# The second token block's operand sums in their usual slot, and one more pair of squares on VectorE, in a two-layer encoder kernel

## Chip, core and metric

The kernel runs on one core of one Trainium2 chip. The metric is the device time of one execution in microseconds (us). The time before is the median of three runs, 934.64 us (934.29 to 935.21). Inside a core five engines work side by side, each through its own instructions in the order in which they were written: TensorE (PE in the profile; PEld is its weight load), VectorE (DVE), ScalarE (ACT), GpSimd (POOL) and SyncE (SP, which here only issues transfers). They meet at semaphores alone.

## What is computed

A two-layer encoder trunk on x (512 tokens, 1024 channels), all in fp32, with cross-attention into 256 memory tokens in each layer. The change lies in the start of the first layer, in front of and inside its first product of the normalised x with the input weights. The reference, cut to that:

```python
def rmsnorm(x, g):
    xf = x.astype(jnp.float32)
    y = xf * lax.rsqrt(jnp.mean(xf * xf, axis=-1, keepdims=True) + EPS)
    return (y * g.astype(jnp.float32)).astype(x.dtype)

for i in range(DEPTH):
    h = rmsnorm(x, norm_g[i])
    mem_h = rmsnorm(mem, mem_norm_g[i])
    ...
    proj = jnp.einsum('bsd,de->bse', h, w_in_a[j])     # layer 0
    ...
    o_mem = memory_attention(q_mem, mem_h, w_mem_kv[i], mem_qn_g[i], mem_kn_g[i])
    y = jnp.concatenate([o_mix, o_mem], axis=-1) * jax.nn.silu(gate)
    x = x + jnp.einsum('bse,ed->bsd', y, w_out[i])
```

## The kernel before

**Products.** Every fp32 product is made of three products of rounded operands: each operand is split into a high part (a cast to fp32r) and a low part (the operand minus its high part), and high by high, low by high and high by low are summed in PSUM (`mm_early`, lines 178 and 179, and `mm_late`, line 182). The high part of a weight, `wh`, is a cast on ScalarE (L333; L331 with gains), its low part, `wo`, a subtraction on VectorE (L347; L345 with gains). Both stand in rings of four buffers. Large products are done by Strassen's scheme in Winograd's form: instead of the four quarters of an operand, seven combinations of quarters are multiplied. Those of x are called 12, 11, S1, S2, S4, S3 and 22, in the order of use, and those of the weights 21, 11, T1, T2, 22, T3 and T4. T1 is summed on VectorE (L291), T2 by a transfer that adds T1 into the loaded quarter (L296, issued by POOL).

**x.** The 512 tokens lie in four blocks, `xb[0]` to `xb[3]` (the tiles x_79 to x_82), each with two halves of 512 channels. A block gets its mean square (`norm_1`: two squares with an accumulated sum, L574 on VectorE or L576 on ScalarE, and three small operations on POOL, L578, L535 and L536) and its factor and gain (`norm_2`, L583, VectorE). Blocks 0 and 1 are the upper quarters, 2 and 3 the lower ones. For c = 0 and c = 1, blocks c and 2 + c are transposed on TensorE into the banks of `at` and combined: `first_t` makes 12 and 11 of block c, `diffs_t` makes S1, S3 and keeps 22 of block 2 + c, and `rest_t` makes S2 = S1 - 11 (L675, tile `f11`) and S4 = 12 + S2 (L677, tile `f12`), then writes the two parts of S2, S4, S3 and 22 (`put`: cast L671, subtraction L672). c = 0 and c = 1 are the left and the right 128 columns of one operand tile such as `hS2`.

**Order.** `Driver` is a hand-made schedule. A slot is one group of eight early and four late matmuls. After each slot, tasks whose turn has come run to their next `yield n`, and so put a few instructions on the engines; n is the number of slots to their next turn. What is given to `late` is written at the end of the same slot, what is given to `release` with a delay of one in the next slot, at the point where PSUM banks are handed over (`drv.free()`, behind the group's matmuls and ahead of the weights' work in `W.advance()`). The task `prep` (L1213 on) norms and transposes x; its two tasks `forms(0)` and `forms(1)`, the second one slot behind, run `diffs_t` and `rest_t`.

**Banks.** The product with S2 is added onto the banks that hold the product with 11 (`pj_596` for c = 0, `pj_597` for c = 1). Before that VectorE must have read them into `sn` (L438, the sum for output quarter 11). These two sums are called the banks' sums here.

**Transfers.** SP issues the weights' transfers (L260) in the order of use. Eight semaphores go round, so a transfer is issued only when the one that had its semaphore before has landed.

Of the kernel before, what the change touches and what calls it, by code (L numbers as in the profile page):

```python
# [10 lines left out]
F32 = mybir.dt.float32  # L11
F32R = mybir.dt.float32r
AF = mybir.ActivationFunctionType
ALU = mybir.AluOpType
# [119 lines left out]
def trunk_kernel(ctx: ExitStack, tc: tile.TileContext, x, mem, wall, norm_g, mem_norm_g, gcol,  # L134
                 qn_a, kn_a, qn_b, kn_b, ident_d, mask_d, tab_a, tab_b, out):
    nc = tc.nc
    V, A, G, T = nc.vector, nc.scalar, nc.gpsimd, nc.tensor
# [6 lines left out]
    drv = Driver()  # L144
# [7 lines left out]
    def s2(dt=F32, name="s2"):  # L152
        return pool.tile([128, 512], dt, tag="s2", name=name, bufs=NS2)
# [7 lines left out]
    def sm(n, name):  # L161
        return small.tile([128, n], F32, tag="sm%d" % n, name=name)
# [368 lines left out]
    def rstd_of(ss, n):  # L531

        r = sm(n, "rstd")
        e = sm(n, "mse")
        G.tensor_scalar(e, ss, EPS, None, ALU.add)  # L535
        G.tensor_tensor(r, e, half[:, 0:n], ALU.pow)  # L536
        return r
# [30 lines left out]
    def norm_1(xb, both=False):  # L568

        ss = sm(2, "ss")  # L570
        for j in range(2):
            jk = s2(name="sq")
            if both and j:
                V.tensor_tensor_reduce(jk, xb[j], xb[j], 1.0 / 1024.0, 0.0, ALU.mult, ALU.add, ss[:, j:j + 1])  # L574
            else:
                A.activation(jk, xb[j], AF.Square, scale=1.0 / 32.0, accum_out=ss[:, j:j + 1])  # L576
        r, e = sm(1, "rstd"), sm(1, "mse")
        G.tensor_tensor(e, ss[:, 0:1], ss[:, 1:2], ALU.add)  # L578
        return rstd_of(e, 1)

    def norm_2(xb, r, row, js=(0, 1)):
        for j in js:
            V.scalar_tensor_tensor(xb[j], xb[j], r, row[j], ALU.mult, ALU.mult)  # L583
# [44 lines left out]
    def slot(H, k, c):  # L628
        if c == 0:
            part[k] = big(F32R, "h" + k).rearrange("p (a k t) -> p a k t", a=2, k=4)  # L630
        else:
            H[k] = part[k]
        cs = slice(c * 128, (c + 1) * 128)
        return part[k][:, 0, :, cs], part[k][:, 1, :, cs]
# [9 lines left out]
    def first_t(H, top, c, view=same, turn=same):  # L644

        ps = [(k, turn(turn4(top[j], None, None)), [view(t) for t in slot(H, k, c)]) for k, j in (("12", 1), ("11", 0))]
        for k, p, hl in ps:
            split(*hl, p)
        for k, p, _ in ps:
            A.copy(view(whole(k, c)), p)  # L650

    def diffs_t(H, low, c, view=same, turn=same, late=False):

        f22 = whole("22", c)
        A.copy(view(f22), turn(turn4(low[1], None, None)))
        p = turn(turn4(low[0], None, None))
        yield 1
        s1, s3 = whole("S1", c), whole("S3", c)
        V.tensor_tensor(view(s1), p, view(f22), ALU.subtract)
        V.tensor_tensor(view(s3), view(full["11", c]), p, ALU.subtract)  # L660
        hl = slot(H, "S1", c)
        if late:
            drv.late(lambda: split(*hl, s1))
        else:
            split(*hl, s1)

    def rest_t(H, c, ds, spread=False):

        def put(k, f):
            hi, lo = slot(H, k, c)  # L670
            A.copy(hi, f)  # L671
            (drv.soon if spread and c and k == "S2" else drv.late)(lambda: V.tensor_tensor(lo, f, hi.bitcast(F32), ALU.subtract))  # L672

        s1, s2_, s4, s3, f22 = [full.pop((k, c)) for k in ("S1", "11", "12", "S3", "22")]
        V.tensor_tensor(s2_, s1, s2_, ALU.subtract)  # L675
        if not spread:
            V.tensor_tensor(s4, s4, s2_, ALU.add)  # L677
        put("S2", s2_)
        if spread:
            yield ds[0] - 1  # L680
            V.tensor_tensor(s4, s4, s2_, ALU.add)
            yield 1
        else:
            yield ds[0]
        put("S4", s4)
        yield ds[1]
        put("S3", s3)
        yield ds[2]
        put("22", f22)
        yield 1  # L690
# [24 lines left out]
    def halves(t):  # L715
        return [t[:, 0:512], t[:, 512:1024]]
# [489 lines left out]
    H, H2 = {}, {}  # L1206
# [4 lines left out]
    xb = [halves(t) for t in xt]  # L1211

    n = {}  # L1213

    def prep():

        for c in range(5):
            if c > 2:
                norm_2(xb[c - 1], n[c - 1], rows["x"])
            if 1 < c < 4:  # L1220
                n[c] = norm_1(xb[c], c == 2)
            if 1 < c < 4:
                first_t(H, xb[c - 2], c - 2, by_class, from_rows)
            yield 1

        def forms(c):
            yield from diffs_t(H, xb[2 + c], c, by_class, from_rows, late=True)
            yield 3 + c
            yield from rest_t(H, c, (2 - c, 2, 2))

        drv.spawn(forms(1), 1)
        yield from forms(0)
# [70 lines left out]
    def ahead(u, b):  # L1303

        if (u, b) == (0, 0):
            square(1, 0)
            place_m(1, 0)
            square(0, 1, False)
            W.hi(True)
            W.hi(True)  # L1310
        if (u, b) == (0, 1):
            place_m(0, 1)
            factor(0)
            square(1, 1, False)
            place_m(1, 1)
            n[0] = norm_1(xb[0])
            n[1] = norm_1(xb[1])
            factor(1)
        if (u, b) == (1, 0):
            norm_2(xb[0], n[0], rows["x"])  # L1320
            norm_2(xb[1], n[1], rows["x"])

    drv.spawn(prep(), PD)
    drv.spawn(setup(), SET_AT)
    drv.spawn(masks(), MASK_AT)
# [436 lines left out]
    last_k, both = [], [v[:, :, 256:512] for v in kbT]  # L1762
# [219 lines left out]
```

## Time and profile before

| | |
|---|---|
| median of three runs | 934.64 us |
| the profiled execution's own time | 934.81 us |
| its span in the profile | 933.0 us |
| DVE busy | 800.5 us, 86% of the span |
| ACT busy | 696.6 us, 75% |
| POOL busy | 360.9 us, 39% |
| granted TensorE clock | 1.00 in the whole span |

The 1.8 us between time and span lie ahead of the first and behind the last instruction. A row of the timeline has the start in us, the length in us, engine, line, operation, output <- input, and the count; in brackets it has the idle time just before it and what ended that. The ends of matmuls are modelled and overlap the next start, so what TensorE loses is read from starts.

### The profile page before, as it was taken

The numbers are of one execution on the slowest core, as the hardware profiler recorded it, in microseconds if no ns is written. First come the engines' busy times: TensorE is split into PE (matmuls) and PEld (weight loads), VectorE is DVE, ScalarE is ACT, GpSimd is POOL, SyncE is SP. The second block draws the span as 40 slices with busy tenths as digits, with TensorE's granted clock in tenths as the row PEclk, the third lists the DMA queues.
The fourth block names the chain that finished last, engine by engine and source line by source line (L and its number), as shares of the span: only waits on it lengthen the run. The fifth ranks groups of instructions, "written<-read, shape, count | busy, mean of one in ns | idle before, by whom it ended". The sixth has DMA issues, their size and how long they took to land.

```text
span 933.0 us, 16277 instructions
## 1 busy us (share of the span) xinstructions
PE 925.0 (99%) x5471; PEld 814.4 (87%) x5471; DVE 800.5 (86%) x1453; ACT 696.6 (75%) x1729; POOL 360.9 (39%) x504
## 2 busy tenths in 40 slices
PE   9999999999999999999999999999999999999998
PEld 7879888888888888888889998888988999999886
DVE  6898677878888888979798989999898998789977
ACT  7775789686868686767676767757878887789774
POOL 4411424557564646463746102234252440110122
PEclk9999999999999999999999999999999999999999
DMA  9999947968686868685867899999995677785777
GB/s 349 390 269 331 292 128 191 333 149 243 158 254 158 266 159 272 157 270 115 259 168 213 229 256 274 288 317 330 298 220 114 173 229 187 198 228 116 197 165 181
DMA packets 83179, 212.85 MB, mean 228 GB/s; under 512 B 18960, under 2 KB 25752, under 8 KB 83096
## 3 DMA queue, kind: packets, MB, share of 16 engines
q1 hardware_dynamic: 60744, 141.16, 41.9%
q0 software_dynamic: 20384, 67.12, 39.0%
q10 hardware_dynamic: 1968, 3.54, 1.0%
q8 instruction: 43, 0.70, 0.3%
q14 instruction: 40, 0.33, 0.1%
HBM read 162.96 MB, written 12.65 MB: 188 GB/s over the span
## 4 chain that ended last, share of the span: by engine, by line
PE 88%; DVE 5%; DMA 4%; issue 1%; ACT 1%; POOL 0%; SPq 0%; DVEq 0%; POOLq 0%; ACTq 0%
PE pj L179 23%; PE pj L178 23%; PE pj L182 23%; PE qT L708 2%; DMA wl<-in_wall_dram 2%; PE sa L1468 2%; PE oo L1577 2%; PE ptb L1811 1%; PE sa L1464 1%; DVE wo L347 1%; PE pt L1556 1%; DMA x<-in_x_dram 1%; DMA wl<-wl 1%; PE ob L178 1%; PE ob L182 1%
## 5 line engine op out<-in xcount | busy, mean ns | idle before, releaser
L347 DVE TENSOR_TENSOR wo<-wl,wh 128x1024 fp32r<-128x1024 f32 x253 | 308.5, 1224 | 5.5 <-ACT wh L333 5.5
L333 ACT CAST wh<-wl 128x1024 fp32r<-128x1024 f32 x253 | 267.1, 1061 | 30.5 <-PE pj L179 18.9
L178 PE MATMUL pj<-wh,hS 128*128 128x512 f32 (+1 forms) x416 | 154.6, 380 | 1.1 <-ACT hS L671 1.1
L179 PE MATMUL pj<-wh,hS 128*128 128x512 f32 (+1 forms) x416 | 148.9, 367 | 0.3 <-DVE hS L672 0.3
L178 PE MATMUL pj<-wh,h 128*128 128x512 f32 (+1 forms) x312 | 115.3, 378 | 0.0
L179 PE MATMUL pj<-wh,h 128*128 128x512 f32 (+1 forms) x312 | 111.6, 366 | 0.0
L536 POOL TENSOR_TENSOR rstd<-mse,half 128x4 f32<-128x4 f32 (+2 forms) x98 | 101.9, 1040 | 8.2
L182 PE MATMUL pj<-wo,hS 128*128 128x512 f32 (+1 forms) x416 | 99.4, 365 | 0.0
L178 PEld LDWEIGHTS pj<-wh,hS 128*128 128x128 f32 x416 | 78.6, 189 | 12.5 <-ACT hS L671 1.5
L179 PEld LDWEIGHTS pj<-wh,hS 128*128 128x128 f32 x416 | 78.7, 189 | 11.7 <-DVE hS L672 0.6
L535 POOL TENSOR_SCALAR mse<-hss 128x4 f32<-128x4 f32 (+1 forms) x88 | 45.0, 512 | 109.7 <-ACT junk L696 96.8
L182 PEld LDWEIGHTS pj<-wo,hS 128*128 128x128 f32 x416 | 72.5, 189 | 12.8
L696 ACT ACTIVATE junk<-sn 128x128 f32<-128x128 f32 x264 | 79.3, 310 | 2.5 <-DVE sn L428 2.5
L260 POOL DMA_DIRECT2D wl<-in_wall_dram x44 | 42.0, 983 | 94.5 <-DMA wl<-in_wall_dram 34.2
L1409 POOL TENSOR_TENSOR ta<-sn,tabs 128x128 f32<-128x128 f32 (+1 forms) x64 | 38.2, 604 | 104.0 <-DVE sn L701 80.4
L415 ACT COPY sn<-pj 128x512 f32<-128x512 f32 x122 | 67.2, 590 | 12.3 <-PE pj L182 12.3
L182 PE MATMUL pj<-wo,h 128*128 128x512 f32 (+1 forms) x312 | 74.5, 365 | 0.0
L306 POOL DMA_DIRECT2D wl<-wl x35 | 31.0, 895 | 108.2 <-DVE wo L347 48.9
L438 DVE TENSOR_TENSOR sn<-pj,sn 128x512 f32<-128x512 f32 x89 | 60.7, 683 | 7.2 <-PE pj L182 6.9
L179 PEld LDWEIGHTS pj<-wh,h 128*128 128x128 f32 x312 | 59.0, 189 | 8.4
L178 PEld LDWEIGHTS pj<-wh,h 128*128 128x128 f32 x312 | 59.0, 189 | 8.2
L296 POOL DMA_DIRECT2D wl<-wl x35 | 32.9, 974 | 78.1 <-PE pj L179 16.8
(299 smaller groups left out, 2402.5 us busy)
## 6 DMA issues: line engine op xcount, KB each, us to landing
wl<-in_wall_dram SPq DMA_DIRECT2D x226, 512.0 KB, 7.4
wl<-wl POOLq DMA_DIRECT2D x70, 512.0 KB, 5.8
wl<-in_wall_dram POOLq DMA_DIRECT2D x48, 512.0 KB, 8.6
od<-o SPq DMA_DIRECT2D x9, 256.0 KB, 5.7
x<-in_x_dram SPq DMA_DIRECT2D x4, 512.0 KB
v0r<-sn SPq DMA_DIRECT2D x8, 256.0 KB, 8.6
v0d<-v0r SPq DMA_DIRECT2D x4, 512.0 KB
og<-od ACTq DMA_DIRECT2D x4, 512.0 KB
```

The source lines that it names most:

```text
L178: T.matmul(o, a, b, start=start, stop=False, skip_group_check=True)
L179: T.matmul(o, c, d, start=False, stop=False, skip_group_check=True)
L182: T.matmul(o, a, b, start=False, stop=stop, skip_group_check=True)
L260: queue.dma_start(t, wall[d], **how)
L333: A.copy(wh, self.tile[key])
L347: V.tensor_tensor(wo, self.tile[key], wh.bitcast(F32), ALU.subtract)
L415: A.copy(t_, b_)
L438: V.tensor_tensor(t_, b_, t_, ALU.subtract if q == "12" and late is None else ALU.add)
L535: G.tensor_scalar(e, ss, EPS, None, ALU.add)
L536: G.tensor_tensor(r, e, half[:, 0:n], ALU.pow)
L696: A.activation(jk, p[:, j * 128:(j + 1) * 128], AF.Square, scale=by, accum_out=ss[:, j:j + 1])
L1409: G.tensor_tensor(ta[:, 0:n], xn[:, 0:n, 0:32], ropeA[:, 0, b, s0:s0 + n], ALU.mult)
```

## The change

Three edits, all in the first layer's start:

1. Both halves of x's fourth block (`xb[3]`) are squared on VectorE (L574) and not on ScalarE (L576), and at the same turn as those of the third block, one turn earlier than before.
2. `forms(1)` waits three slots, as `forms(0)` does, between `diffs_t` and `rest_t`, where it waited four, and then two slots, where it waited one, before it writes S4. S2 and its sums for c = 1 so come one slot earlier; S4, S3 and 22 stay where they were.
3. The low part of S2 for c = 1 is written by a task that is released in the next slot, behind the banks' sums, and not at the end of its own slot.

```diff
@@ norm_1 @@
-            if both and j:
+            if both and (j or both == 2):
                 V.tensor_tensor_reduce(jk, xb[j], xb[j], 1.0 / 1024.0, 0.0, ALU.mult, ALU.add, ss[:, j:j + 1])
@@ rest_t @@
         def put(k, f):
             hi, lo = slot(H, k, c)
             A.copy(hi, f)
-            (drv.soon if spread and c and k == "S2" else drv.late)(lambda: V.tensor_tensor(lo, f, hi.bitcast(F32), ALU.subtract))
+
+            def low():
+                V.tensor_tensor(lo, f, hi.bitcast(F32), ALU.subtract)
+                yield 1
+
+            if c and k == "S2" and not spread:
+                drv.release(low(), 1)
+            else:
+                (drv.soon if spread and c and k == "S2" else drv.late)(lambda: next(low()))
@@ prep @@
             if c > 2:
                 norm_2(xb[c - 1], n[c - 1], rows["x"])
-            if 1 < c < 4:
-                n[c] = norm_1(xb[c], c == 2)
+            if c == 2:
+                n[2], n[3] = norm_1(xb[2], 1), norm_1(xb[3], 2)
...
         def forms(c):
             yield from diffs_t(H, xb[2 + c], c, by_class, from_rows, late=True)
-            yield 3 + c
-            yield from rest_t(H, c, (2 - c, 2, 2))
+            yield 3
+            yield from rest_t(H, c, (2, 2, 2))
```

In the changed file the lines behind `put` have numbers that are 8 higher: L675 is L683 there, L701 is L709, and L672 is L674.

On VectorE, at the turn of the third block's squares (x_81 is the third block, x_82 the fourth; each square is two rows, the second of which reads the accumulator), before:

```order
L345 SCALAR_TENSOR_TENSOR wo_298<-wl_108,gmc_70,wh_297 128x512 x2
L574 ISA sq_363,ss_360<-x_81 128x512
L574 ISA ss_360 128x1
L169 TENSOR_TENSOR h12_377<-xT_372,h12_377 128x4x128
L169 TENSOR_TENSOR h11_383<-xT_378,h11_383 128x4x128
L345 SCALAR_TENSOR_TENSOR wo_353<-wl_114,gmc_70,wh_352 128x512 x2
```

and at the same place after:

```order
L345 SCALAR_TENSOR_TENSOR wo_298<-wl_108,gmc_70,wh_297 128x512 x2
L574 ISA sq_363,ss_360<-x_81 128x512
L574 ISA ss_360 128x1
L574 ISA sq_373,ss_372<-x_82 128x512
L574 ISA ss_372 128x1
L574 ISA sq_375,ss_372<-x_82 128x512
L574 ISA ss_372 128x1
L169 TENSOR_TENSOR h12_389<-xT_384,h12_389 128x4x128
```

Two squares of the fourth block now stand ahead of the low parts of 12 and 11 for c = 0. On ScalarE the two L576 rows of x_82, ahead of the casts of 12 and 11 for c = 1, are gone.

On VectorE, at the end of the products with S1 (f11 and f12 with the smaller number are c = 0, those with 456 and 454 are c = 1; wo_641 is the low part of the first weight piece of T2, which the S2 product uses), before:

```order
L347 TENSOR_TENSOR wo_617<-wl_214,wh_616 128x1024
L438 TENSOR_TENSOR sn_610<-pj_596,sn_610 128x512
L438 TENSOR_TENSOR sn_612<-pj_597,sn_612 128x512
L347 TENSOR_TENSOR wo_641<-wl_216,wh_640 128x1024
L675 TENSOR_TENSOR f11_456<-fS1_574,f11_456 128x512
L677 TENSOR_TENSOR f12_454<-f12_454,f11_456 128x512
L672 TENSOR_TENSOR hS4_666<-f12_388,hS4_666 128x4x128
L672 TENSOR_TENSOR hS2_623<-f11_456,hS2_623 128x4x128
L347 TENSOR_TENSOR wo_664<-wl_218,wh_663 128x1024
```

and after:

```order
L347 TENSOR_TENSOR wo_617<-wl_214,wh_616 128x1024
L683 TENSOR_TENSOR f11_456<-fS1_574,f11_456 128x512
L685 TENSOR_TENSOR f12_454<-f12_454,f11_456 128x512
L438 TENSOR_TENSOR sn_610<-pj_596,sn_610 128x512
L438 TENSOR_TENSOR sn_612<-pj_597,sn_612 128x512
L674 TENSOR_TENSOR hS2_623<-f11_456,hS2_623 128x4x128
L347 TENSOR_TENSOR wo_641<-wl_216,wh_640 128x1024
L674 TENSOR_TENSOR hS4_670<-f12_400,hS4_670 128x4x128
L347 TENSOR_TENSOR wo_668<-wl_218,wh_667 128x1024
```

The sums of c = 1 now stand ahead of the banks' sums, and the low part of S2 for c = 1 between these and wo_641.

On ScalarE at the same place (wh_640 and wh_663, after the change wh_667, are the high parts of the two pieces of T2), before:

```order
L671 CAST hS2_623<-f11_390 128x4x128
L333 CAST wh_640<-wl_216 128x1024
L333 CAST wh_663<-wl_218 128x1024
L671 CAST hS4_666<-f12_388 128x4x128
L671 CAST hS2_623<-f11_456 128x4x128
```

and after:

```order
L671 CAST hS2_623<-f11_402 128x4x128
L333 CAST wh_640<-wl_216 128x1024
L671 CAST hS2_623<-f11_456 128x4x128
L333 CAST wh_667<-wl_218 128x1024
L671 CAST hS4_670<-f12_400 128x4x128
```

The cast of S2 for c = 1 now stands ahead of the cast of T2's second piece.

## Prediction

> **What bounds the kernel now.** I read the page first, then the waits of TensorE, then the timelines of the engines around each wait.
>
> ```profile
> PE 925.0 (99%) x5471; PEld 814.4 (87%) x5471; DVE 800.5 (86%) x1453; ACT 696.6 (75%) x1729; POOL 360.9 (39%) x504
> PE 88%; DVE 5%; DMA 4%; issue 1%; ACT 1%; POOL 0%; SPq 0%; DVEq 0%; POOLq 0%; ACTq 0%
> ```
>
> TensorE is busy for 99% of the span, and the change adds no product and takes none away. So it can only gain where TensorE waits. The list of its waits in the whole span is short:
>
> ```profile
> PE pj L178 <- ACT hS L671: 1.1, 1, 1.1
> ...
> PE xT L589 <- ACT h L166: 0.5, 1, 0.5
> PE pj L179 <- DVE hS L672: 0.3, 1, 0.3
> ```
>
> The change touches the surroundings of these three. The first and third stand together:
>
> ```profile
> 49.65 0.39 PE L178 MATMUL pj<-wh,hS 128*128 128x512 f32 x1
> ...
> 51.47 1.08 PE L182 MATMUL pj<-wo,hS 128*128 128x512 f32 x4
> ...
> 52.74 0.48 PE L178 MATMUL pj<-wh,hS 128*128 128x512 f32 x1
> ...
> 54.98 0.50 PE L178 MATMUL pj<-wh,hS 128*128 128x512 f32 x1 [1.06 <-ACT hS L671]
> 55.79 0.50 PE L179 MATMUL pj<-wh,hS 128*128 128x512 f32 x1 [0.31 <-DVE hS L672]
> ...
> 56.61 1.08 PE L182 MATMUL pj<-wo,hS 128*128 128x512 f32 x4
> ```
>
> The group at 49.65 ran unhindered: 1.82 us from its first matmul to its late ones. The S2 group began at 52.74, so its late ones were due at 54.56, or about 54.64 (the first matmul behind transposes is followed some 0.08 us later than usual). They came at 56.61. **The stall is 1.97 us**, more than the 1.06 + 0.31 of the list, because modelled ends overlap. That is all that this place can give.
>
> Why it stalls is seen on ScalarE and VectorE:
>
> ```profile
> 48.81 1.06 ACT L333 CAST wh<-wl 128x1024 fp32r<-128x1024 f32 x1
> 52.84 1.05 ACT L333 CAST wh<-wl 128x1024 fp32r<-128x1024 f32 x1 [2.97 <-DMA wl<-wl]
> 53.80 1.13 ACT L671 CAST hS<-f 128x512 fp32r<-128x512 f32 x2
> ...
> 49.42 1.22 DVE L347 TENSOR_TENSOR wo<-wl,wh 128x1024 fp32r<-128x1024 f32 x1
> 50.56 1.28 DVE L438 TENSOR_TENSOR sn<-pj,sn 128x512 f32<-128x512 f32 x2
> 51.76 1.21 DVE L347 TENSOR_TENSOR wo<-wl,wh 128x1024 fp32r<-128x1024 f32 x1
> 52.89 0.68 DVE L675 TENSOR_TENSOR f<-fS,f 128x512 f32<-128x512 f32 x1
> 53.61 0.69 DVE L677 TENSOR_TENSOR f<-f,f 128x512 f32<-128x512 f32 x1
> 54.44 1.29 DVE L672 TENSOR_TENSOR hS<-f,hS 128x512 fp32r<-128x512 f32 x2
> ```
>
> S2 for c = 1 is computed at 52.89, and its cast is the second of the two at 53.80, behind a cast that waited 2.97 us for T2's second piece to land. Its low part is the second of the two at 54.44 and ends at 55.73; TensorE goes on at 55.79, 0.06 us later.
>
> **Part 1: S2 one slot earlier (edits 2 and 3).** The same VectorE instructions stand in a new order. Behind the low part at 49.42 (1.14 us from start to start): S2's sum 50.56, S4's sum 51.28 (0.72 later, as at 52.89 and 53.61), the two banks' sums 51.93 and 52.53 (0.65 on, the usual step behind that sum, then 0.60 each), S2's low part 53.13, wo_641 53.74, which ends 1.21 us later at 54.95. ScalarE's cast now stands ahead of the wait: ScalarE is free at 49.87, so the cast runs at about 51.3 and ends at 51.9, far ahead of the 53.75 at which TensorE's c = 1 half is due, four matmuls behind 52.74. Taken one by one, TensorE's needs are: the first bank's sum by 52.74 (it ends at about 52.6), S2's low part by about 53.98 (53.82), and wo_641 by 54.64 (54.95 + 0.06 = 55.01). **So the wait moves from S2 to wo_641**, and without more the late matmuls start at 55.01 and not at 56.61: 1.60 us are won, 0.37 stay.
>
> **Part 2: the squares (edit 1).** VectorE and ScalarE before:
>
> ```profile
> 23.60 0.68 DVE L574 CUSTOM_DVE_ANT_0 sq<-x 128x512 f32<-128x512 f32 x1
> 24.21 0.08 DVE L574 DVE_READ_ACCUMULATOR2_ANT ss<- 128x1 f32 x1
> 25.98 1.29 DVE L169 TENSOR_TENSOR h<-xT,h 128x512 fp32r<-128x512 f32 x2 [1.69 <-ACT h L166]
> ...
> 29.83 1.41 DVE L583 SCALAR_TENSOR_TENSOR x<-x,rstd,row 128x512 f32<-128x512 f32 x2
> 31.16 1.28 DVE L169 TENSOR_TENSOR h<-xT,h 128x512 fp32r<-128x512 f32 x2
> 32.64 1.44 DVE L583 SCALAR_TENSOR_TENSOR x<-x,rstd,row 128x512 f32<-128x512 f32 x2 [0.20 <-POOL rstd L536]
> ...
> 29.17 0.65 ACT L576 ACTIVATE sq<-x 128x512 f32<-128x512 f32 x1
> ...
> 30.39 1.08 ACT L166 CAST h<-xT 128x512 fp32r<-128x512 f32 x2
> ```
>
> ScalarE loses 30.39 - 29.17 = 1.22 us of work, VectorE gains two squares at 0.61 each from start to start (23.60 to 24.21), in the 1.69 us in which it sat idle for ScalarE's cast. The cover is tight, because the fourth block must have landed. SP shows when:
>
> ```profile
> SPq L260 <- DMA x<-in_x_dram: 0.9, 1, 0.9
> 24.76 0.33 SPq L260 DMA_DIRECT2D wl<-in_wall_dram  x1
> ```
>
> That weight transfer has the semaphore of the fourth block's transfer, so the block landed at about 24.75. The squares run from 24.78 to 26.00, and the low parts start at about 26.02 where they started at 25.98. **Cost: 0.04 us**, and every us by which the block lands later goes on to the norm at 29.83, since VectorE has no idle time in between, and from there to TensorE:
>
> ```profile
> 29.89 1.07 PE L182 MATMUL pj<-wo,act 128*128 128x512 f32 x4
> 31.50 1.06 PE L589 MATMUL xT<-ident,x 128*128 128x128 f32 x8 [0.55 <-ACT h L166]
> ```
>
> The transposes at 31.50 turn the third block, which VectorE's norm hands over at 29.83 + 1.41 = 31.24. The list names ScalarE's cast, which ends at 31.47; but in the code the transposes read x and take banks whose copies ended by 28, and have no use for that cast. I take VectorE as the true releaser, so this stall, 0.70 us (31.50 against 29.89 + 0.91, four late matmuls), is not removed by freeing ScalarE.
>
> What the squares give is the 0.20 us at 32.64: the fourth block's factor needs 1.2 us on POOL, and with the sums at 26.0 it is long there. The pair at 31.16 lets the next instruction start after 1.21 us (25.98 to 27.19 in the same pair), so at 32.37: 0.27 us earlier, less the 0.04. VectorE keeps this lead up to the stall, for it has hardly any idle time:
>
> ```profile
> 31.00:54.00 23.00, 22.42 (x108) 18.44 (x108) 22.28 (x29) 15.76 (x23) 7.73 (x12) 1.00 1.04 339
> ```
>
> 22.28 of 23.00 us are busy, and the one wait for ScalarE (0.26 us at 46.30) is for a cast that hangs on VectorE's own sums. So wo_641 ends at 54.95 - 0.23 = 54.72, the late matmuls start at 54.78, **and 1.83 us are won**; 0.10 stay.
>
> The Trainium skill speaks against the squares here: by "GPSIMD Engine Reference", section 1 (Specifications), GpSimd and VectorE contend for SBUF interfaces when a VectorE instruction has two SBUF inputs, as these squares have. It is weighed among the rivals.
>
> **Part 3: what follows.** 1.8 us must still be there at the end. Behind 56 us TensorE waits for nothing in the list. The nearest deadlines:
>
> ```profile
> 55.65 1.22 DVE L347 TENSOR_TENSOR wo<-wl,wh 128x1024 fp32r<-128x1024 f32 x1
> 59.80 1.07 PE L182 MATMUL pj<-wo,hS 128*128 128x512 f32 x4
> 60.00:80.00 20.00, 20.00 (x101) 17.04 (x100) 19.73 (x29) 11.61 (x15) 2.66 (x3) 1.00 1.05 309
> ```
>
> The next low weight part ends at 56.87 and is used at 59.80, 2.9 us later, and VectorE reaches it some 0.2 us earlier now. VectorE is full to 80 us (19.73 of 20), so the 1.8 us come off such margins first. Much later there is one more place where VectorE is full, and the chain of waits runs over ScalarE and VectorE there from 719.70 to 770:
>
> ```profile
> 719.70 0.59 ACT L842 CAST pmT<-pmt 128x512 fp32r<-128x512 f32 x1 [0.18 <-PE pmt L839]
> ```
>
> Its first link was idle and released by TensorE, so the stretch begins earlier by what TensorE is ahead. I cost Part 3 at nothing; without that cover up to the whole 1.8 us is lost.
>
> **Sum.** -1.60 (S2 earlier) - 0.23 (VectorE's lead) = -1.83. TensorE itself comes 0.04 us later to the S2 group, which the lead contains already. Against the profiled execution: 934.81 - 1.83 = 932.98. This execution was 0.17 us above the median, so a median should show 932.8; I say **932.9**. Without any lead it is 933.2, with the stall gone entirely 932.7 to 932.8.
>
> **Rivals.**
>
> - *The list is right about the stall at 31.50.* Then the casts, 1.22 us earlier, end it: another 0.70 us, 932.2. For it speaks that the cast ends 0.03 us ahead of the transposes, against it the code.
> - *The gain is used up later*: VectorE or a transfer is late next where TensorE no longer is. Then 934.6, or between. For it speak VectorE's full stretches at 60 and 720 us and transfers at a share of 1.05 at 60 to 80 us; against it that TensorE never waits there and that 2.9 us is more than 1.8.
> - *GpSimd holds the squares up.* Each square would wait for POOL's operation, up to 26.72, when POOL has the third block's factor; the squares would end near 27.3, 1.3 us late, and TensorE at 31.50 with them: 934.3.
>
> ```profile
> 23.17 1.21 POOL L535 TENSOR_SCALAR mse<-hss 128x4 f32<-128x4 f32 x1
> 26.15 0.57 POOL L536 TENSOR_TENSOR rstd<-mse,half 128x1 f32<-128x1 f32 x1
> 88.67 0.30 POOL L535 TENSOR_SCALAR mse<-hss 128x4 f32<-128x4 f32 x1 [2.03 <-ACT junk L696]
> ```
>
>   Against it: the square at 23.60 ran inside POOL's operation and took its 0.68. It was POOL that paid, 1.21 against 0.30 for the same operation later. Of the skill's rule the trace so far agrees with the contention, at POOL's cost; POOL's factor for the third block, ready at 26.72 and needed at 29.83, can bear that.
> - *Slower: the squares wait for the fourth block.* VectorE stands in order, so the low parts of 12 and 11, four weight parts and the norm wait behind a square whose data isn't there. The price is one for one from a landing at 24.75 on; at 1.8 us the gain is gone, and 0.2% slower takes a landing 3.7 us later, at 28.4, or 936.5. The transfer's place in the queue is unchanged, which speaks against it.
>
> **Chances.** 0.2% of 934.64 is 1.87 us, about what a measurement of this kernel can tell from no change, so the forecast lies right at that bound. Forecast (932.6 to 933.4): 0.66, of which I give 0.27 to faster and 0.39 to the same. The stall at 31.50 goes too: 0.11, faster. Used up later: 0.14, the same. GpSimd: 0.03, the same. Slower mechanism: 0.06, of which 0.01 is the same. That is 0.38 faster, 0.57 same, 0.05 slower. The range reaches over the first two cases and into the third, 932.0 to 934.3.
>
> **What would show it.** In the profile after: no wait of TensorE at S2's c = 1 half, at most some 0.1 us ahead of the late matmuls; L178 to L182 of that group in about 2.0 us and not 3.9; VectorE's norm of the fourth block at about 32.4 without a wait for POOL; the transposes still at about 31.5. I am wrong in Part 2 if these start near 30.8, or if a square starts well behind 24.8; and in Part 3 if TensorE has a new wait behind 56 us.

## The result, and the profile after

The changed kernel takes 933.50 us (median of 22 executions, 932.81 to 935.08), the kernel before 935.02 us in the same series (22 executions, 934.29 to 936.85). The ratio is 0.9986, with a 95% interval of 0.9980 to 0.9992. The forecast was 932.9 us, in a range of 932.0 to 934.3. The profiled execution has a span of 931.4 us, where it had 933.0.

From the page of the changed kernel, the engines' busy time and the chain that ended last:

```profile
PE 924.8 (99%) x5471; PEld 814.7 (87%) x5471; DVE 801.7 (86%) x1457; ACT 695.7 (75%) x1725; POOL 360.5 (39%) x504
PE 91%; DVE 5%; DMA 2%; ACT 1%; SPq 0%; issue 0%; DVEq 0%; ACTq 0%
```

VectorE has four more instructions (two squares with their two reads of the accumulator), ScalarE four fewer, and TensorE the same 5471. TensorE's waits in the changed kernel (in total, how often, the longest):

```profile
PE xT L589 <- DVE x L583: 1.0, 1, 1.0
PE idle L1298 <- POOL tabs L550: 1.0, 1, 1.0
PE pj L179 <- DVE act L169: 0.2, 1, 0.2
```

Both waits for S2 are gone. The wait ahead of the third block's transposes is still there, and is now put down to VectorE's norm. The S2 group on TensorE in the changed kernel:

```profile
52.53 0.60 PE L716 MATMUL qT<-ident,xn 128*128 128x128 f32 x4
52.89 0.48 PE L178 MATMUL pj<-wh,hS 128*128 128x512 f32 x1
...
53.90 0.39 PE L178 MATMUL pj<-wh,hS 128*128 128x512 f32 x1
54.13 0.39 PE L179 MATMUL pj<-wh,hS 128*128 128x512 f32 x1
...
54.82 1.16 PE L182 MATMUL pj<-wo,hS 128*128 128x512 f32 x4
55.83 0.60 PE L716 MATMUL qT<-ident,xn 128*128 128x128 f32 x4
```

The c = 1 half (53.90 and 54.13) follows its predecessors without a gap, and from the group's first matmul to its late ones it is 1.93 us, where it was 3.87. The late matmuls take 1.01 us to the next start and not 0.92 as before (56.61 to 57.53): about 0.1 us of the stall is left in them. VectorE at the same place in the changed kernel:

```profile
49.26 1.22 DVE L347 TENSOR_TENSOR wo<-wl,wh 128x1024 fp32r<-128x1024 f32 x1
50.39 0.69 DVE L683 TENSOR_TENSOR f<-fS,f 128x512 f32<-128x512 f32 x1
51.11 0.69 DVE L685 TENSOR_TENSOR f<-f,f 128x512 f32<-128x512 f32 x1
51.72 1.28 DVE L438 TENSOR_TENSOR sn<-pj,sn 128x512 f32<-128x512 f32 x2
52.92 0.68 DVE L674 TENSOR_TENSOR hS<-f,hS 128x512 fp32r<-128x512 f32 x1
53.52 1.22 DVE L347 TENSOR_TENSOR wo<-wl,wh 128x1024 fp32r<-128x1024 f32 x1
```

S2's sum, S4's sum, the banks' sums, S2's low part and wo_641 (53.52) stand in the order that was worked out ahead, and wo_641 ends at 54.74, 0.08 us before the late matmuls start.

### The profile page after: what moved, and what is told of

The parts are those of the page before. It is cut to its first block, busy times and chain, and to the rows that moved or that the text cites. A ratio compares the mean times of both kernels' runs of the same rounds, so it can differ in the third digit from the quotient of the medians.

```text
span 931.4 us, 16276 instructions
## 1 busy us (share of the span) xinstructions
PE 924.8 (99%) x5471; PEld 814.7 (87%) x5471; DVE 801.7 (86%) x1457; ACT 695.7 (75%) x1725; POOL 360.5 (39%) x504
## 4 chain that ended last, share of the span: by engine, by line
PE 91%; DVE 5%; DMA 2%; ACT 1%; SPq 0%; issue 0%; DVEq 0%; ACTq 0%
PE pj L178 24%; PE pj L179 24%; PE pj L182 24%; PE qT L716 3%; PE sa L1476 2%; PE oo L1585 2%; PE ptb L1819 1%; PE sa L1472 1%; DVE wo L347 1%; PE pt L1564 1%; DMA x<-in_x_dram 1%; DMA row<-in_norm_g_dram 1%; PE ob L178 1%; PE ob L182 1%; PE ob L179 1%; PE xT L589 1%
## 5 line engine op out<-in xcount | busy, mean ns | idle before, releaser
L178 PE MATMUL pj<-wh,hS 128*128 128x512 f32 (+1 forms) x416 | 154.5, 380 | 0.0
L178 PE MATMUL pj<-wh,h 128*128 128x512 f32 (+1 forms) x312 | 115.3, 378 | 0.0
L182 PE MATMUL pj<-wo,hS 128*128 128x512 f32 (+1 forms) x416 | 99.5, 366 | 0.0
L178 PEld LDWEIGHTS pj<-wh,hS 128*128 128x128 f32 x416 | 78.6, 189 | 11.0
L182 PEld LDWEIGHTS pj<-wo,hS 128*128 128x128 f32 x416 | 72.4, 189 | 13.0 <-DVE wo L347 0.2
L182 PE MATMUL pj<-wo,h 128*128 128x512 f32 (+1 forms) x312 | 74.5, 366 | 0.0
L178 PEld LDWEIGHTS pj<-wh,h 128*128 128x128 f32 x312 | 59.0, 189 | 8.2
```

What stands on the lines that cost most here:

```text
L178: T.matmul(o, a, b, start=start, stop=False, skip_group_check=True)
L182: T.matmul(o, a, b, start=False, stop=stop, skip_group_check=True)
```

## Experiments: which edit gives the gain

Ten kernels ran. The times of each series stand against runs of the kernel before on the same chip (934.82 us in the first two series, 934.89 in the third); the changed kernel's first 22 executions stand against the 935.02 of their own series. The ratio lies close to that of the means and not of the medians, so a few late executions raise it. Theory A is that of the prediction: the sums' order (edits 2 and 3) gives most of the gain, and the squares (edit 1) give VectorE a small lead. Theory B is that freeing ScalarE gives it; C, that the place of the low part alone does.

**The sums alone.** Edits 2 and 3, with the squares as before.

```diff
-            if c == 2:
-                n[2], n[3] = norm_1(xb[2], 1), norm_1(xb[3], 2)
+            if 1 < c < 4:
+                n[c] = norm_1(xb[c], c == 2)
```

> The sums' two edits alone, the squares as before. Theory A (the sums' order gives the gain, the squares only a small lead of VectorE, bought with a dependence on the landing of x's fourth block): transposes of the third block at 31.5 as before, S2's late matmuls wait some 0.35 us for the weight's low part, 1.6 us below the kernel before, about as fast as the changed kernel's median, with fewer single runs a us above its fastest. Theory B (freeing ScalarE of two squares gives the gain): no faster than before.

**The squares alone.** Edit 1, with the old slots for `rest_t` and S2's low part at the end of its own slot.

```diff
-            if c and k == "S2" and not spread:
+            if False:
...
-            yield 3
-            yield from rest_t(H, c, (2, 2, 2))
+            yield 3 + c
+            yield from rest_t(H, c, (2 - c, 2, 2))
```

> The squares' edit alone. Theory A: the stall in the S2 group stays, at most 0.3 us shorter because VectorE's lead makes T2's second piece land earlier; within 0.3 us of before. Theory B: 1 to 1.5 us below before, as the changed kernel.

**The low part ahead of the banks' sums.** Edits 1 and 2 without 3.

```diff
-            if c and k == "S2" and not spread:
+            if False:
```

> The changed kernel with S2's low part for c = 1 written in its own slot, ahead of the banks' sums. Theory A: the first bank's sum ends at about 53.05 and not 52.4, so the S2 group starts 0.2 us later; VectorE's low weight part is at the same time as in the changed kernel: 0.05 to 0.2 us above the changed kernel. Theory C (the place of the low part is what matters, ScalarE's cast order is not): back near before, over 1 us above the changed kernel.

**The third block's squares on VectorE in place of the fourth's.** The sums' edits stay. Both squares of the third block, which lands earlier, are on VectorE, and both of the fourth on ScalarE, behind its copies for c = 0.

```diff
-                n[2], n[3] = norm_1(xb[2], 1), norm_1(xb[3], 2)
+                n[2] = norm_1(xb[2], 2)
             if 1 < c < 4:
                 first_t(H, xb[c - 2], c - 2, by_class, from_rows)
+            if c == 2:
+                n[3] = norm_1(xb[3])
```

> The sums' edits, both squares of the third block on VectorE, both of the fourth on ScalarE behind the copies of 12 and 11 for c = 0. Theory A (the stall at 31.6 is VectorE's, set by the landing of the fourth block through the squares and by ScalarE's square ahead of its cast): VectorE's low parts of 12 and 11 start at about 25.5 and not 26.1, the transposes at about 31.0, no wait in the S2 group: 0.5 to 0.7 us below the changed kernel, and single runs closer together. Rival D (the transposes wait for ScalarE's casts for c = 1, as the list of before had it): no earlier than 31.6, since these casts come 0.6 us later.

Read from TensorE's timelines: the start of the third block's transposes (L589), of the S2 group (its first L178) and of its late matmuls (L182), and the way, which is the time from the transposes to the late matmuls and does not contain what was lost or won ahead of the transposes:

| kernel | L589 | S2 group | L182 | way | median (lowest to highest), us | ratio to before, 95% interval |
|---|---|---|---|---|---|---|
| before | 31.50 | 52.74 | 56.61 | 25.11 | 934.82 | |
| changed | 31.64 | 52.89 | 54.82 | 23.18 | 933.50 (932.81 to 935.08) | 0.9986 (0.9980 to 0.9992) |
| sums alone | 31.66 | 52.91 | 55.13 | 23.47 | 933.96 (933.43 to 936.13) | 0.9995 (0.9986 to 1.0003) |
| squares alone | 31.49 | 52.72 | 56.14 | 24.65 | 934.79 (934.18 to 938.04) | 1.0001 (0.9992 to 1.0010) |
| low part first | 31.40 | 52.97 | 54.89 | 23.49 | 933.82 (933.16 to 934.40) | 0.9988 (0.9980 to 0.9997) |
| third block on VectorE | 30.79 | 51.97 | 53.98 | 23.19 | 933.32 (932.81 to 938.29) | 0.9992 (0.9981 to 1.0002) |

On the way, theory A holds: the sums alone shorten the way by 25.11 - 23.47 = 1.64 us, the squares alone by 0.46 (more than the 0.3 expected, and not to be seen in the time), and on top of the sums by 23.47 - 23.18 = 0.29. B falls: the squares alone leave both waits for S2. C falls too: without edit 3 the way is only 0.31 longer, though that is more than expected. Each row rests on one profile, but the way comes out alike where it should: 23.17 to 23.19 in three other profiles of the changed kernel's start (the control and the two kernels with the scaling of grA moved, all below), and 25.07 in the kernel before with its scaling moved.

The times say less. Of these kernels only the changed one and the one with the low part first have an interval that leaves out 1. The sums alone are 0.86 us below the kernel before in the medians, where 1.6 were expected, and their interval reaches over 1. Four of their 11 executions lie over 1 us above their fastest, about the share of the changed kernel (9 of 22), where fewer were expected.

Where the 0.31 us of the kernel with the low part first go is seen on its VectorE:

```profile
51.53 0.69 DVE L674 TENSOR_TENSOR hS<-f,hS 128x512 fp32r<-128x512 f32 x1
52.14 1.28 DVE L438 TENSOR_TENSOR sn<-pj,sn 128x512 f32<-128x512 f32 x2
```

and on its TensorE:

```profile
52.28 0.60 PE L716 MATMUL qT<-ident,xn 128*128 128x128 f32 x4
52.97 0.47 PE L178 MATMUL pj<-wh,hS 128*128 128x512 f32 x1
```

The banks' sums come behind the low part, and the S2 group starts 0.69 us after the transposes ahead of it, where it starts 0.36 after them in the changed kernel (52.53 to 52.89). The list of waits names nothing here; only the starts show it.

The fourth kernel shows who sets the start of the third block's transposes. VectorE and ScalarE in it:

```profile
25.00 1.29 DVE L169 TENSOR_TENSOR h<-xT,h 128x512 fp32r<-128x512 f32 x2 [0.43 <-ACT h L166]
26.21 2.73 DVE L345 SCALAR_TENSOR_TENSOR wo<-wl,gmc,wh 128x512 fp32r<-128x512 f32 x4
28.86 1.41 DVE L583 SCALAR_TENSOR_TENSOR x<-x,rstd,row 128x512 f32<-128x512 f32 x2
...
29.41 1.09 ACT L166 CAST h<-xT 128x512 fp32r<-128x512 f32 x2
```

VectorE's low parts, weight parts and norm all come about 1.1 us earlier than in the changed kernel (26.12 and 29.97 there), the transposes run at 30.79 without a wait, right behind the late matmuls ahead of them (29.87 + 0.91), and ScalarE's cast of 12 and 11 for c = 1 still starts at 29.41 (29.30 in the changed kernel) and ends at 30.50. In the changed kernel the same cast was done at 30.39, and the transposes still came only at 31.64, behind the norm. So the norm sets the transposes there. At the late matmuls TensorE is 56.61 - 53.98 = 2.63 us ahead of the kernel before, but the span is 931.1 us, only 1.9 shorter: 0.7 us is used up later, where no wait of TensorE is listed. The starts show the places: ahead of the changed kernel it is 0.79 us at the late matmuls at 68.19, 0.55 at those at 71.15, and 0.37 at the transposes at 101.02. The median is hardly below that of the changed kernel, where 0.5 to 0.7 us were expected, and single executions lie no closer together. That is the rival of a gain used up later, seen at a lead of 2.6 us and not at 1.8.

## Experiments: does the fourth block's landing decide?

In the changed kernel the fourth block's landing stands at the head of the chain to the transposes. VectorE there:

```profile
23.07 0.69 DVE L574 CUSTOM_DVE_ANT_0 sq<-x 128x512 f32<-128x512 f32 x1
...
24.86 0.69 DVE L574 CUSTOM_DVE_ANT_0 sq<-x 128x512 f32<-128x512 f32 x1 [1.10 <-DMA x<-in_x_dram]
...
25.48 0.69 DVE L574 CUSTOM_DVE_ANT_0 sq<-x 128x512 f32<-128x512 f32 x1
...
26.12 1.29 DVE L169 TENSOR_TENSOR h<-xT,h 128x512 fp32r<-128x512 f32 x2
...
29.97 1.41 DVE L583 SCALAR_TENSOR_TENSOR x<-x,rstd,row 128x512 f32<-128x512 f32 x2
31.30 1.28 DVE L169 TENSOR_TENSOR h<-xT,h 128x512 fp32r<-128x512 f32 x2
32.50 1.41 DVE L583 SCALAR_TENSOR_TENSOR x<-x,rstd,row 128x512 f32<-128x512 f32 x2
```

To see whether an earlier landing would bring the transposes forward, the block's transfer was issued ahead of one weight transfer that it stands behind:

```diff
-    W.dma(2)
+    W.dma(1)
     nc.sync.dma_start(xt[3], xv[3])
+    W.dma(1)
```

> The changed kernel, with the transfer of x's fourth block issued ahead of the second of the two weight transfers that it stood behind. Theory H (the landing of the fourth block, 24.84 us in the changed kernel's profile, now sets the start of the transposes of the third block at 31.64): its squares follow those of the third block at about 23.8, and the transposes start at 30.6 to 30.9, 0.7 to 1.0 earlier. Theory A (ScalarE's casts of the last weight pieces, L331 x4, end at 24.9 and its casts of 12 and 11 for c = 1 at 26.5, so VectorE has the low parts no more than 0.1 earlier, whatever the block does): the transposes move by less than 0.2 from the block alone, and since the weight piece now lands about 1.3 later, ScalarE's casts and with them the low parts and the transposes come 0.5 to 1.2 later, 32.1 to 32.8; median 933.9 to 934.6.

The edit also puts that weight transfer behind the block. The kernel takes 934.82 us (933.76 to 935.72), ratio 0.9998 (0.9989 to 1.0007): the whole gain is lost. VectorE and ScalarE in this kernel:

```profile
24.48 0.69 DVE L574 CUSTOM_DVE_ANT_0 sq<-x 128x512 f32<-128x512 f32 x1
25.09 0.08 DVE L574 DVE_READ_ACCUMULATOR2_ANT ss<- 128x1 f32 x1
27.20 1.29 DVE L169 TENSOR_TENSOR h<-xT,h 128x512 fp32r<-128x512 f32 x2 [2.03 <-ACT h L166]
...
24.75 1.34 ACT L331 ACTIVATE wh<-wl,gmc 128x512 fp32r<-128x512 f32 x2 [1.98 <-PE xT L589]
```

The squares end 1.0 us earlier than in the changed kernel (25.17 against 26.17), and VectorE then waits 2.03 us for ScalarE, whose weight cast comes late. The list puts that cast down to TensorE, but the delayed weight piece is what it uses next, and SP, whose next transfer takes that piece's semaphore, goes on at 24.71, where it went on at 23.64 in the changed kernel: 1.07 us later. The transposes start at 32.72, 1.08 us later, as theory A had it, and the time is 0.2 us above its bound. In this profile the late matmuls of S2 come 2.72 us later (57.54); the other 1.6 us are lost behind 32.7, where the granted clock is 0.60 (last section).

Since the edit moves two transfers, it doesn't tell by itself what the block does. The sums alone do, for there VectorE squares nothing of the fourth block. ScalarE's casts of 12 and 11 for c = 0 in the kernel before, in the changed kernel and in the sums alone, and VectorE's low parts in the last:

```profile
25.38 1.05 ACT L166 CAST h<-xT 128x512 fp32r<-128x512 f32 x2
...
25.52 1.05 ACT L166 CAST h<-xT 128x512 fp32r<-128x512 f32 x2
...
25.54 1.05 ACT L166 CAST h<-xT 128x512 fp32r<-128x512 f32 x2
26.14 1.29 DVE L169 TENSOR_TENSOR h<-xT,h 128x512 fp32r<-128x512 f32 x2 [2.39 <-ACT h L166]
```

The low parts start 0.60 us behind the start of these casts in all three (at 25.98, 26.12 and 26.14), with the squares or without them. So theory H falls: in the changed kernel the squares (done at 26.17) and ScalarE's first of these casts meet, and an earlier block alone would win nothing there. What a later one costs, no run here shows.

## Experiments: why the times of the changed kernel fall into two groups

Of its 22 executions 13 lie between 932.81 and 933.55 us and 9 between 934.02 and 935.08. In the profile of the kernel with the squares alone (938.04 us) VectorE stands at L1263, the scaling of the gains grA, which two small loads bring (48 KB each; SP issues them at 53.83 and 54.30):

```profile
72.48 0.21 DVE L1263 TENSOR_SCALAR grA<-grA 128x96 f32<-128x96 f32 x1 [3.06 <-DMA grA<-in_qn_a_dram]
```

and TensorE soon after it:

```profile
71.79 0.39 PE L179 MATMUL pj<-wh,h 128*128 128x512 f32 x1
74.04 0.47 PE L178 MATMUL pj<-wh,h 128*128 128x512 f32 x1 [1.86 <-DVE sn L438]
...
75.21 1.91 PE L182 MATMUL pj<-wo,h 128*128 128x512 f32 x4
```

VectorE works in order, so a bank's sum behind L1263 is late and TensorE stops for it. The kernel with the low part first (its profiled execution took 934.18 us) stands there too. VectorE there, and TensorE some 13 us later:

```profile
71.86 0.21 DVE L1263 TENSOR_SCALAR grA<-grA 128x96 f32<-128x96 f32 x1 [3.04 <-DMA grA<-in_qn_a_dram]
84.19 0.68 DVE L438 TENSOR_TENSOR sn<-pj,sn 128x512 f32<-128x512 f32 x1
...
83.16 1.12 PE L182 MATMUL pj<-wo,hS 128*128 128x256 f32 x8
84.93 0.39 PE L178 MATMUL pj<-wh,hS 128*128 128x256 f32 x1 [0.65 <-DVE sn L438]
```

The changed kernel's profile reaches L1263 at 68.93 and does not wait. Its VectorE is at the same bank's sum at 81.35, 2.84 us earlier, so the wait of 3.04 us is hardly made up in between; and its TensorE takes 0.96 us from the same late matmuls to the next start, where it is 1.77 here. So one wait at L1263 costs TensorE some 0.8 us at this place. Theory F is that this wait, in some executions, makes the second group. Rival G is that the group comes from other transfers or from the chip. The use of grA is far behind its scaling, so the scaling was moved, with the four small instructions ahead of it and nothing else:

```diff
@@ setup: the scaling four slots later @@
-        yield 4
+        yield 8
...
-        yield 6
+        yield 2
```

> The changed kernel, with the scaling of the gains grA (VectorE, L1263, which waits for the two small loads of them) written four slots later; the two products that use it stay in their slot. Theory F (in some executions VectorE stands at L1263 for the gains' landing, up to 3 us, TensorE stops behind it for some 1 to 2 us, and this is what splits the changed kernel's times into 932.8 to 933.6 and 934.0 to 935.1): no wait in front of L1263 and, of 11 executions, at most one above 933.9; median 933.0 to 933.3. Rival G (the spread comes from the transfers of x's blocks or of the weights, or from the chip): the spread stays, a third of the executions above 934.0, median 933.4 to 933.6.

The same two lines in the kernel before:

> The kernel before, with the same scaling four slots later. Theory F: the kernel before reaches the scaling about 1 us later than the changed one and its loads are issued up to 4 us later in the profiled run, so it too stands there in some executions: median 934.4 to 934.8, none above 935.3. Rival G: as the kernel before, 934.7 to 935.1 with some at 935.5 and more.

And in the kernel with the third block on VectorE:

> The sums' edits, both squares of the third block on VectorE and both of the fourth on ScalarE (as in e4_third_on_vector), and the scaling of grA four slots later. Theory F: the executions of e4 at 934.5, 935.6 and 938.3 do not come again, median 932.8 to 933.1, the fastest of all kernels here. Rival G: 933.2 to 933.4 with a third above 934, as in e4.

Then the opposite, a larger dose (`yield 2` and `yield 8` in place of 4 and 6), beside the changed kernel once more as its control:

> The changed kernel, with the scaling of grA (L1263) two slots earlier, at about 64 us instead of 68.93, the products that use it in their slot as before: a larger dose of the suspected wait. Theory F (late landings of the gains' loads split the changed kernel's times): more executions stand at L1263, at least 6 of 11 above 934.0, median 934.2 to 936; if the profile shows the wait, it ends at 64 to 72 us and gives the landing. Rival G (the spread has nothing to do with L1263): the share above 934.0 stays at about 4 of 10, median 933.3 to 933.7.

> The changed kernel itself, as the control on the same chip and against the same runs of the kernel before. Theory F and rival G alike: 933.2 to 933.7, with 3 to 6 of 11 executions above 934.0, as in its first 22. If none is above 934.0, the split belongs to the chip or the hour, and the runs of e7_scaling_late prove nothing about L1263.

| kernel | median (lowest to highest), us | above 934.0 | ratio to before, 95% interval |
|---|---|---|---|
| changed, first series | 933.50 (932.81 to 935.08) | 9 of 22 | 0.9986 (0.9980 to 0.9992) |
| changed again (control) | 933.03 (932.76 to 934.63) | 3 of 11 | 0.9983 (0.9974 to 0.9991) |
| changed, scaling later | 933.29 (932.76 to 933.78) | 0 of 11 | 0.9983 (0.9974 to 0.9992) |
| changed, scaling earlier | 937.50 (934.24 to 941.70) | 12 of 12 | 1.0033 (1.0014 to 1.0053) |
| before, scaling later | 934.77 (934.45 to 935.30) | all | 1.0000 (0.9991 to 1.0009) |
| third block on VectorE, scaling later | 933.23 (932.72 to 936.67) | 1 of 11 | 0.9986 (0.9977 to 0.9995) |

Two slots earlier, every execution is long. VectorE in the profiled one (934.51 us):

```profile
66.83 0.21 DVE L1263 TENSOR_SCALAR grA<-grA 128x96 f32<-128x96 f32 x1 [2.70 <-DMA grA<-in_qn_a_dram]
```

The median, 937.50, is above the 934.2 to 936 expected, and the control's, 933.03, below its 933.2 to 933.7.

Four slots later, with the scaling at 78.67 and no wait ahead of it, none of 11 is long. If 12 of 33, as in the changed kernel's runs together, is taken as the true share, none of 11 would come up with a chance of (21/33)^11 = 0.7%. The dose ran on one chip with its control (12 of 12 against 3 of 11). The removal ran on another chip, with the kernel before beside it but not the changed kernel, so for the removal a difference of chips is not excluded. Dose and removal both go with F and against G. This is shown by counts and by the profiles of three sibling kernels; no execution of the changed kernel's own second group was profiled.

Two things F does not give. In the kernel before, the later scaling changed nothing that can be told apart. And the kernel of the last row still had one execution at 936.67 us, with a granted clock of 0.997: such rare ones, over 2 us above the rest, have a further cause that stays open. That kernel also missed its expected 932.8 to 933.1. The later scaling takes the long executions away from the changed kernel without making the short ones shorter, so its median cannot be told from that of the control, and against the kernel before it gains no more: 934.82 - 933.29 = 1.53 us, where the changed kernel's first series has 1.52.

## Why the prediction came out as it did

**Part 1, S2 one slot earlier: right, with its size.** It said 1.60 us; the sums alone shorten the way by 1.64. The wait moved from S2 to wo_641 as worked out: in the sums alone wo_641 ends at 55.08, and the late matmuls start at 55.13. The forecast put the banks' sums, less the lead of 0.23, at 51.70, S2's low part at 52.90 and the end of wo_641 at 54.72; they came at 51.72, 52.92 and 54.74. It could be close because VectorE is full there, so steps from start to start could be carried from one order to the other. That it came within 0.02 us is luck: VectorE's lead at the weight part ahead of these sums was 0.16 us (49.26 against 49.42) and not 0.23, and the steps from there to wo_641 took 4.26 us and not 4.32.

**Part 2, the squares: right in mechanism.** The lead of 0.23 us was measured as 0.29 on top of the sums. The fourth block's factor is there in time: the norm at 32.50 has no wait for POOL, where 0.20 us stood before, and the step from the third block's norm to it is 2.53 us where it was 2.81 (29.83 to 32.64), 0.28 shorter where 0.27 was forecast. The cost ahead of the transposes was given as 0.04, and none can be seen. The transposes start 0.14 us later than before (31.64 against 31.50), but so they do in the sums alone (31.66), where VectorE has no square of the fourth block, and with the squares alone they start at 31.49. What came later are the two weight transfers ahead of the block, whose pieces ScalarE casts before 12 and 11: SP goes on with the semaphore of the second at 23.50 before, at 23.64 in the changed kernel and at 23.66 in the sums alone. So the mechanism of the "slower" rival did not show.

**The stall at 31.50.** The rival that took the list at its word, another 0.70 us, did not come about. ScalarE's casts came 1.1 us earlier (29.30) and the transposes did not follow; the kernel with the third block on VectorE then moved the norm by 1.1 us and the casts by 0.1, and they did. The choice of VectorE as the true releaser is shown.

**GpSimd.** The squares were not held up; each took 0.69. GpSimd beside them, in the changed kernel:

```profile
25.70 0.53 POOL L578 TENSOR_TENSOR mse<-ss 128x1 f32<-128x1 f32 x1 [0.71 <-ACT sq L576]
...
27.16 0.20 POOL L578 TENSOR_TENSOR mse<-ss 128x1 f32<-128x1 f32 x1
```

The same operation took 0.53 us beside a square and 0.20 later beside other work of VectorE (one instance of each); as the prediction had it, GpSimd pays, and can bear it.

**Part 3, carried to the end: right, for these 1.8 us.** The transposes behind the late matmuls start at 55.83 in the changed kernel. TensorE's rows for them and for the last matmuls of all, in the kernel before:

```profile
57.53 0.60 PE L708 MATMUL qT<-ident,xn 128*128 128x128 f32 x4
...
928.42 0.61 PE L182 MATMUL pj<-wo,yl 128*128 128x512 f32 x2
```

and the last matmuls in the changed kernel:

```profile
926.73 0.61 PE L182 MATMUL pj<-wo,yl 128*128 128x512 f32 x2
```

The lead is 57.53 - 55.83 = 1.70 us at the first place and 1.69 at the last: nothing is used up on the way in this execution.

**The 0.6 us between 932.9 and 933.50.** The kernel before was itself at 935.02 in this series, 0.38 above the 934.64 that the forecast started from. The other 0.22 us is a gain of 1.52 us in the medians where 934.64 - 932.9 = 1.74 was forecast. The interval of the ratio, 0.8 to 1.9 us, holds both, so this difference is within the noise, and its cause stays open.

What Part 3 missed is another thing. It said "I cost Part 3 at nothing" after looking for the nearest deadlines among the weights' parts, and the two small loads of grA, on which VectorE waits in order at 69 us, were not among them. By the counts above this transfer is late in about a third of the executions, and in the first series these are some 1.2 us longer. That the lead brings this on is not shown: the squares alone, only 0.47 us ahead at the late matmuls (56.61 - 56.14), stood there for 3.06 us. Nor does it make up the 0.22 us by itself: with the scaling moved and no long execution the gain in the medians is 1.53 us, and in the control series, with 3 of 11 long, it is 1.86. The 13 short executions of the first series alone have a median of 933.18, 1.84 below before, but that leaves out the long ones on one side only.

## What to carry to other kernels

Where an engine is full, work out a new order from start to start of its rows, and ask for each product operand when it is there; a wait that is removed shows at once which operand is late next. Check who a transposition or a product really reads before believing the named releaser. When a chain gets faster, look down each in-order engine for small transfers that were only just in time, since one profile may show them landed and other executions not.

## What the runs showed of the hardware

**Small loads can take long, and not the same time twice.** The two loads of grA were issued at 53.83 and 54.30 us in the kernel with the squares alone, and VectorE could go on at 72.48, 18 us later; in the kernel with the earlier scaling they were issued at 55.68 and 56.18 and had landed by 66.83, 11 us later. SP's row for the second issue is itself 4.62 and 4.48 us long. A weight transfer of 512 KB takes 7.4 to 7.5 us in the median.

**TensorE's clock fell after some 2 us of idle time.** In the kernel with the squares alone, TensorE stood idle for about 2.0 us ahead of 74.04 (the start of 71.79 and its usual 0.23). The windows of that kernel (for each engine the busy time and the instructions, then the granted clock, the transfers' share and GB/s):

```profile
70.00:74.00 4.00, 2.18 (x10) 1.48 (x8) 1.52 (x4) 2.02 (x3) 0.00 (x0) 1.00 1.04 332
74.00:78.00 4.00, 3.96 (x11) 3.19 (x12) 4.00 (x5) 1.04 (x1) 0.83 (x1) 0.60 1.03 413
78.00:82.00 4.00, 4.00 (x25) 3.50 (x25) 3.10 (x5) 1.05 (x1) 0.05 (x1) 0.97 1.06 334
```

The clock is 0.60 for the next 4 us, and four late matmuls take 1.71 us (75.21 to 76.92) instead of 0.91. The kernel with the earlier fourth block shows the same:

```profile
33.00:37.00 4.00, 4.00 (x16) 3.48 (x15) 4.00 (x7) 3.89 (x6) 0.29 (x2) 0.60 1.02 409
```

There four late matmuls spread from 29.57 to the transposes at 32.72, idle for 3.15 - 0.91 = 2.24 us. In the changed kernel the idle time at this place is 31.64 - 29.40 - 0.91 = 1.33 us, and its clock stays at 1.00; in the kernel with the earlier scaling it is 32.06 - 29.70 - 0.91 = 1.45 us, at 1.00 too. So in these profiles idle times up to 1.45 us left the clock alone, and 2.02 us and more did not, by one execution each. The Trainium skill ("TensorE: Matmul & The Clock Gate", Part 1, What's actually happening) gives an idle window of some 3.4 us as what halves the clock; these rows show it after less, and the measurement decides. A wait can so cost more than its length: in the kernel with the squares alone TensorE is 0.47 us ahead of the kernel before at the late matmuls of S2 and 3.23 us behind it at its last matmuls (931.65 against 928.42), a loss of 3.70 us around 2.02 us of idle time. The times with the earlier scaling fit: of the twelve executions six lie between 934.24 and 935.06 us at a mean clock of 0.999 to 1.000, and the other six between 939.93 and 941.70 at 0.996. The six long ones were not profiled, so that they hold such a stretch is likely and not shown.
